# One tile for all weight buffers, plain and Strassen weights at different offsets

## The chip, the cores and the metric

The kernel runs on one core of a Trainium2 chip. The metric is the device time of one execution in microseconds; a kernel's time is the median of several runs. The engines are named as in the profile: PE multiplies matrices (its weight loads are PEld), ACT and DVE work on whole tiles, POOL is a slower third one, SP issues DMAs. Names such as L172 are lines of the kernel before, unless the text says that they are of the changed one.

## The reference

A streaming encoder of two layers, 512 tokens, width 1024, all in float32. Cut to what matters:

```python
def swiglu(x, w_gate, w_up, w_down):            # D_FF = 2816
    return (jax.nn.silu(x @ w_gate) * (x @ w_up)) @ w_down

for l in range(DEPTH):                           # DEPTH = 2
    x = x + 0.5 * swiglu(rms_norm(x, ffn1_norm[l]), ffn1_w_gate[l], ffn1_w_up[l], ffn1_w_down[l])
    h = rms_norm(x, mix_norm[l])
    p = h @ w_in[l]                              # 384 + 256 + 32 + 1024 columns
    attn = mla_group(...)                        # 8 heads, chunk-causal, low-rank q and kv
    conv = conv_group(...)                       # GLU, causal depthwise conv of 31, LayerNorm, silu
    x = x + jnp.concatenate([attn, conv], axis=-1) @ w_out[l]
    x = x + 0.5 * swiglu(rms_norm(x, ffn2_norm[l]), ffn2_w_gate[l], ffn2_w_up[l], ffn2_w_down[l])
    x = rms_norm(x, post_norm[l])
```

## The kernel before, in words

**Products in three parts.** TensorE takes the operands in a rounded form (fp32r). To keep float32's accuracy each operand is split into a high part (the rounded value) and a low part (what rounding left), and each product is three matmuls that add up in one bank: high weights by high activations (L172), high weights by low activations (L173), low weights by high activations (L174), in `mm3`. A weight tile holds 128 partitions by up to 1024 columns, that is 8 blocks of 128 by 128; each block is loaded as PE's stationary operand while the matmul before streams its activations.

**Weights.** A plain weight tile is loaded to a buffer `raw` by SP's queue, cast to the high part on ACT (L153 in `load_w`, L1117 for the first tiles), and the low part is the difference, made on DVE (L159, L1118), for the output projection on POOL or by ACT and an adding DMA. The buffers come from the pool `wpool` by tags, each tag a ring of its own: `raw` (3 buffers), `wh` (4), `wl` (4), of 4 KB a partition each. Two tiny tags, `gap0` of 16 floats and `gap1` of 32, lie between them, allocated once where the first tiles are (the expression above `half_w`). By the allocation the start bytes modulo 512 are: activations `r` 192, `raw` 192, `wh` 256, `wl` 384, and 288 for the buffers of the FFN's own pool (`xj`, `xs`, `ls`, `fr`). Any weight buffer of a kind has the same value, since all are multiples of 512 long.

**An FFN** has the gate and up columns in 11 pairs of 128 by 2. The first two pairs are plain: 512 tokens wide, `plain` and `plain_first`. The other nine go through `pair` (L418): one level of Strassen-Winograd on the 2 by 2 quarters of tokens and depth, seven products instead of eight, each 256 tokens wide. The weight sums are made on DVE in float32 (buffers `fr` and `raw`, L426 to L429) and split again: `split_into` casts on ACT (L262) and subtracts on DVE (L264); `summed` (L415) is for quarters that are used as they are, with a low part `ls` that ACT and an adding DMA make (L407, L408). Four of the seven products take `product` (three 256-wide matmuls a block, L172 to L174 by `mm3`); three take `product_joined`, where high and low activations lie side by side in a tile `xj`: one matmul of 512 columns by the high weights (L391), one of 256 by the low weights (L392), which come from `ls` or, for "t3", from `wl`. The pairs go in four chunks (2, 3, 3 and 3 pairs), each followed by its part of w_down: plain for the first chunk (weight tiles of 128 by 512) and the last (128 by 768), Strassen for the two in between (`down`, L479, whose inner `times` uses `split_into` and `summed` too). The mixing block between the FFNs is plain throughout; in its up-projections of keys and values, weights stream past stationary activations.

**What sets the order.** The program is written through a tile framework: it follows reads and writes of each buffer, and a scheduler with a simulated timeline sets each engine's order, unless the program says that one thing is issued after another (`tc.issue_after`). So the order is fixed among the Strassen products (`order["pe"]` puts each behind the one before) and in some places by names ("first", "u0" and others). Before the change neither the casts nor the low parts of weights are held in program order.

Of the kernel before, what the change touches and what calls it, by code (L numbers as in the profile page):

```python
# [7 lines left out]
FP = mybir.dt.float32  # L8
FR = mybir.dt.float32r
# [3 lines left out]
ALU = mybir.AluOpType  # L13
AX = mybir.AxisListType

P = 128
# [16 lines left out]
EPS = 1e-6  # L33
WC = 1024
GAP = 96
HS = S // 2
RING = 35
WIDE = 6
# [11 lines left out]
POOLW = "wo"  # L50
# [29 lines left out]
def encoder_kernel(ctx: ExitStack, tc: tile.TileContext, xT, consts, vecs, rgain, wgu1, wd1, wdq1,  # L80
# [6 lines left out]
    wpool = ctx.enter_context(tc.tile_pool(name="w", bufs=4))  # L87
# [4 lines left out]
    def nm(s):  # L92
        uid[0] += 1
        return f"{s}{uid[0]}"
# [21 lines left out]

    small.tile([P, GAP], FP, tag="gap", name="gap", bufs=1)
    V, A, G, T = nc.vector, nc.scalar, nc.gpsimd, nc.tensor
# [30 lines left out]
    def load_w(src, w, kind=""):  # L149
        raw = wpool.tile([P, WC], FP, tag="raw", name=nm("raw"), bufs=3)  # L150
        nc.sync.dma_start(out=raw[:, :w], in_=src)
        hi = wpool.tile([P, WC], FR, tag="wh", name=nm("wh"))
        order["cast"] = A.copy(hi[:, :w], raw[:, :w]).ins  # L153
        lo = low()
        if kind == "sum":
            A.activation(lo[:, :w], raw[:, :w], AF.Copy, scale=-1.0)
            G.dma_start(out=lo[:, :w], in_=src, accum_op=ALU.add)
            return hi, lo
        (G if kind in POOLW.split() else V).tensor_tensor(lo[:, :w], raw[:, :w], hi[:, :w].bitcast(FP),  # L159
                                                          ALU.subtract)  # L160
        return hi, lo

    def low():
        return wpool.tile([P, WC], FR, tag="wl", name=nm("wl"))

    order = {}

# [90 lines left out]

    def split_into(q, src, w=WC):

        hi = wpool.tile([P, WC], FR, tag="wh", name=nm("wh"))
        A.copy(hi[:, :w], src[:, :w])  # L262
        lo = low()
        order["lo"] = V.tensor_tensor(lo[:, :w], src[:, :w], hi[:, :w].bitcast(FP), ALU.subtract).ins  # L264
        return hi, lo

    def ffn(l, gx, norm, wgu, wd, wdq, gain, done, w0=None, halved=KD):
# [3 lines left out]
    def ffn_body(fpool, l, gx, norm, wgu, wd, wdq, gain, done, w0, halved):  # L271
# [52 lines left out]
        def operands(R):  # L324

            def joined(src):
                both = fpool.tile([P, 2, S], FR, tag="xj", name=nm("xj"), bufs=WIDE)
                A.copy(both[:, :, 0:HS], src)
                V.tensor_tensor(both[:, :, HS:S], src, both[:, :, 0:HS].bitcast(FP), ALU.subtract)
                return both  # L330
# [13 lines left out]
            for i in range(2):  # L344
                e, o = wide(quarter()), wide(quarter())
                for j in range(2):
                    for par, t in ((0, e), (1, o)):
                        m = 4 * i + 2 * j + par
                        V.scalar_tensor_tensor(t[:, j], x[:, m, :], gain[:, m:m + 1], R, ALU.mult, ALU.mult)
                        yield  # L350
                b11, b12, b21, b22 = (v[:, :, h * HS:(h + 1) * HS] for v in (e, o) for h in range(2))
                for n, src in (("b11", b11), ("b21", b21)):
# [21 lines left out]
        def product(o, w, n, start, stop):  # L374
            with tc.issue_after(order["pe"]):
                for gu in range(2):
                    for k in range(4):
                        hi, lo = X[n][k // 2]
                        t = slice(k % 2 * HS, (k % 2 + 1) * HS)
                        c = slice(gu * 512 + k * P, gu * 512 + (k + 1) * P)  # L380
                        last = mm3(o[:, gu * HS:(gu + 1) * HS], w[0][:, c], w[1][:, c], hi[:, t], lo[:, t],
                                   start and gu == 0 and k == 0, stop and k == 3, True)
            order["pe"] = last

        def product_joined(os, w, n, start):
            with tc.issue_after(order["pe"]):
                for gu, o in enumerate(os):
                    for k in range(4):
                        both = X[n][k // 2][:, k % 2]
                        c = slice(gu * 512 + k * P, gu * 512 + (k + 1) * P)  # L390
                        T.matmul(o, w[0][:, c], both, start=start and k == 0, stop=False, skip_group_check=True)  # L391
                        last = T.matmul(o[:, 0:HS], w[1][:, c], both[:, 0:HS], start=False, stop=k == 3,  # L392
                                        skip_group_check=True).ins
# [10 lines left out]
        def subtracted(w, src, n=WC):  # L404

            lo = fpool.tile([P, WC], FR, tag="ls", name=nm("ls"), bufs=2)
            A.activation(lo[:, :n], src[:, :n], AF.Copy, scale=-1.0)  # L407
            G.dma_start(out=lo[:, :n], in_=w, accum_op=ALU.add)  # L408
            return lo

        def summed(w, src, n=WC, lo=None):

            lo = subtracted(w, src, n) if lo is None else lo
            hi = wpool.tile([P, WC], FR, tag="wh", name=nm("wh"))
            A.copy(hi[:, :n], src[:, :n])  # L415
            return hi, lo

        def pair(p, quartered):  # L418
# [121 lines left out]
        for p0, p1 in CHUNKS:  # L540
# [54 lines left out]
            for m in range(halved if last else KD):  # L595
                if m in ahead:
                    pd, w = ahead[m]
# [440 lines left out]
    class Finish:  # L1038
# [37 lines left out]
        def part(self, h, src, first):  # L1076
            for t in range(2):
                i = T.matmul(self.ss[:, 2 * h + t:2 * h + t + 1], src[:, t * P:(t + 1) * P], ones[:, 0:1],
                             start=first and h == 0 and t == 0, stop=not first, skip_group_check=True)
            return i.ins  # L1080
# [26 lines left out]
    st = Stats()  # L1107
    f = gained(0, "g1", gx, first_gain)
    f(0)
    w0 = [tuple(wpool.tile([P, w], t, tag=tag, name=nm(tag), bufs=n) for t, tag, n, w in (  # L1110
        (FP, "raw", 3, WC), (FP, "gap0", 1, 16), (FR, "wh", 4, WC), (FP, "gap1", 1, 32), (FR, "wl", 4, WC)))[::2]
        for _ in range(2)]

    def half_w(q, gu):
        raw, hi, lo = (v[:, gu * 512:(gu + 1) * 512] for v in w0[q])
        nc.sync.dma_start(out=raw, in_=wgu1[0, 0, q, :, gu * 512:(gu + 1) * 512])
        A.copy(hi, raw)  # L1117
        V.tensor_tensor(lo, raw, hi.bitcast(FP), ALU.subtract)  # L1118
    for m in KS:
        if m:  # L1120
            nc.sync.dma_start(out=x[:, m, :], in_=xT[m])
# [6 lines left out]
    w0 = [w[1:] for w in w0]  # L1128
# [172 lines left out]
```

## Time and profile before

| what | value |
|---|---|
| median of 3 runs | 1783.02 us (1781.78 to 1783.49) |
| the profiled run | 1781.53 us |
| span of its trace | 1779.8 us |
| mean granted TensorE clock | 0.999 |
| PE busy | 1768.6 us, 99% |
| PEld busy | 1558.0 us, 88% |
| DVE busy | 1486.0 us, 83% |
| ACT busy | 1094.9 us, 62% |
| POOL busy | 383.3 us, 22% |

In the rows of groups, `out<-in partitions*rows x columns xcount | busy, mean ns | idle before` stands for one line and shape. A row of the timeline is start, duration, engine, line, operation, buffers and shape. Matmuls are pipelined, so durations overlap; the distance from one start to the next is what one costs. The rows of the chain of work give shares of the span by engine and by line.

### The profile page before, as it was taken

The page shows a single profiled execution, that of the slowest core. Times are in us where ns is not written, and L with a number is a line of the kernel's source. Part 1 is how long each engine was busy: PE and PEld are TensorE (multiplying, and loading weights), DVE is VectorE, ACT ScalarE, POOL GpSimd, SP SyncE. Part 2 cuts the span into 40 slices and gives each one's busy share as a digit, 9 for nine tenths or more (in the row PEclk, how much of TensorE's full clock was granted, in tenths as well). Part 3 has the DMA queues.
Part 4 walks back from the last instruction along what each step waited for, and adds up shares of the span by engine and source line. Part 5 has one row for each costly group of instructions (what it writes and reads, how often), then busy time and mean ns, then how long its engine had stood idle before and what let it go on. Part 6 is the DMA issues. An engine that isn't in the chain of part 4 may idle for free.

```text
span 1779.8 us, 29441 instructions
## 1 busy us (share of the span) xinstructions
PE 1768.6 (99%) x11430; PEld 1558.0 (88%) x11430; DVE 1486.0 (83%) x2309; ACT 1094.9 (62%) x1699; POOL 383.3 (22%) x315
## 2 busy tenths in 40 slices
PE   9999999999999999999999999999999999999998
PEld 7899999888678899999888999998976788999997
DVE  7998988588965989998779989876989559999883
ACT  5576766456953575757645757554768435757664
POOL 1000000247822000000310000002576410000002
PEclk9999999999999999999999999999999999999999
DMA  5657574324203466665426575743260125575742
GB/s 170 165 140 186 136 189 114 109 86 124 71 25 101 124 162 162 159 166 131 123 66 167 125 197 124 198 112 112 80 157 24 58 68 155 150 180 140 186 117 74
DMA packets 71947, 228.28 MB, mean 128 GB/s; under 512 B 8448, under 2 KB 9600, under 8 KB 71808
## 3 DMA queue, kind: packets, MB, share of 16 engines
q1 hardware_dynamic: 55536, 171.87, 30.5%
q0 software_dynamic: 16128, 54.53, 18.3%
q8 instruction: 89, 1.46, 0.3%
q14 instruction: 50, 0.41, 0.1%
q10 hardware_dynamic: 144, 0.00, 0.0%
HBM read 222.19 MB, written 2.10 MB: 126 GB/s over the span
## 4 chain that ended last, share of the span: by engine, by line
PE 91%; DVE 5%; ACT 2%; issue 1%; DMA 1%; SPq 0%; ACTq 0%; DVEq 0%
PE ps L172 24%; PE ps L174 24%; PE ps L173 23%; PE ps L391 11%; PE ps L392 6%; DVE cv L972 1%; PE ps L921 1%; DVE mx L880 1%; PE ps L899 1%; DVE wl L264 1%; PE ps L876 0%; PE ps L678 0%; PE ps L216 0%; PE ps L914 0%; DVE r L902 0%
## 5 line engine op out<-in xcount | busy, mean ns | idle before, releaser
L172 PE MATMUL ps<-r,wh 128*128 128x256 f32 (+1 forms) x2556 | 808.8, 320 | 1.7 <-ACT wh L1117 0.6
L173 PE MATMUL ps<-r,wh 128*128 128x256 f32 (+1 forms) x2556 | 807.4, 316 | 0.8 <-DVE r L180 0.4
L174 PE MATMUL ps<-r,wl 128*128 128x256 f32 (+1 forms) x2364 | 753.9, 321 | 0.0
L172 PEld LDWEIGHTS ps<-r,wh 128*128 128x128 f32 x2556 | 480.6, 188 | 51.0 <-issue 3.7
L173 PEld LDWEIGHTS ps<-r,wh 128*128 128x128 f32 x2556 | 480.1, 188 | 42.7 <-DVE r L180 2.5
L174 PEld LDWEIGHTS ps<-r,wl 128*128 128x128 f32 x2364 | 444.1, 188 | 38.5 <-DVE wl L159 0.7
L391 PE MATMUL ps<-xj,wh 128*128 128x512 f32 x864 | 302.5, 390 | 0.0
L153 ACT CAST wh<-raw 128x1024 fp32r<-128x1024 f32 (+3 forms) x148 | 132.4, 900 | 227.9 <-PE ps L173 140.3
L262 ACT CAST wh<-fr 128x1024 fp32r<-128x1024 f32 (+1 forms) x160 | 157.8, 986 | 103.5 <-DVE fr L428 53.2
L159 DVE TENSOR_TENSOR wl<-raw,wh 128x1024 fp32r<-128x1024 f32 (+3 forms) x132 | 142.6, 1089 | 92.5 <-ACT wh L153 91.7
L408 POOL DMA_DIRECT2D ls<-in_wgu x72 | 62.5, 868 | 724.3 <-ACT ls L407 522.5
L264 DVE TENSOR_TENSOR wl<-fr,wh 128x1024 fp32r<-128x1024 f32 (+1 forms) x160 | 182.8, 1143 | 20.2 <-ACT wh L262 20.2
L391 PEld LDWEIGHTS ps<-xj,wh 128*128 128x128 f32 x864 | 160.8, 188 | 29.1
L392 PE MATMUL ps<-xj,ls 128*128 128x256 f32 x576 | 161.3, 280 | 0.0
L978 POOL TENSOR_TENSOR y<-y,pr 128x495 f32<-128x495 f32 (+29 forms) x90 | 120.3, 1339 | 46.6 <-ACT pr L976 41.2
L262 ACT CAST wh<-raw 128x1024 fp32r<-128x1024 f32 (+1 forms) x100 | 97.9, 979 | 42.1 <-PE ps L173 21.1
L264 DVE TENSOR_TENSOR wl<-raw,wh 128x1024 fp32r<-128x1024 f32 (+1 forms) x100 | 113.8, 1138 | 11.8 <-ACT wh L262 11.2
L392 PEld LDWEIGHTS ps<-xj,ls 128*128 128x128 f32 x576 | 108.1, 188 | 0.0
L209 POOL TENSOR_TENSOR r<-r,t 128x512 f32<-128x512 f32 x45 | 75.3, 1681 | 133.3 <-ACT t L205 132.7
L407 ACT ACTIVATE ls<-fr 128x1024 fp32r<-128x1024 f32 (+1 forms) x56 | 56.1, 1001 | 73.3 <-PE ps L392 41.5
L972 DVE SCALAR_TENSOR_TENSOR cv<-m,vec,cv 128x511 f32<-128x511 f32 (+14 forms) x120 | 88.1, 734 | 4.6 <-ACT cv L968 3.0
L408 POOL DMA_DIRECT2D ls<-in_wdq x32 | 27.6, 863 | 258.6 <-ACT ls L407 258.6
(258 smaller groups left out, 2921.5 us busy)
## 6 DMA issues: line engine op xcount, KB each, us to landing
fr<-in_wgu SPq DMA_DIRECT2D x112, 512.0 KB, 4.2
ls<-in_wgu POOLq DMA_DIRECT2D x72, 512.0 KB, 6.6
raw<-in_wgu SPq DMA_DIRECT2D x62, 512.0 KB, 4.6
fr<-in_wdq SPq DMA_DIRECT2D x48, 384.0 KB, 4.7
ls<-in_wdq POOLq DMA_DIRECT2D x32, 384.0 KB, 4.9
raw<-in_wd SPq DMA_DIRECT2D x32, 384.0 KB, 3.2
raw<-in_wd SPq DMA_DIRECT2D x32, 256.0 KB, 2.8
raw<-in_wcv SPq DMA_DIRECT2D x16, 512.0 KB, 3.6
```

What stands on the lines that cost most here:

```text
L153: order["cast"] = A.copy(hi[:, :w], raw[:, :w]).ins
L159: (G if kind in POOLW.split() else V).tensor_tensor(lo[:, :w], raw[:, :w], hi[:, :w].bitcast(FP), ALU.subtract)
L172: T.matmul(o, lh, rh, start=first, stop=False, skip_group_check=free)
L173: T.matmul(o, lh, rl, start=False, stop=False, skip_group_check=free)
L174: order["mm"] = T.matmul(o, ll, rh, start=False, stop=last, skip_group_check=free).ins
L262: A.copy(hi[:, :w], src[:, :w])
L264: order["lo"] = V.tensor_tensor(lo[:, :w], src[:, :w], hi[:, :w].bitcast(FP), ALU.subtract).ins
L391: T.matmul(o, w[0][:, c], both, start=start and k == 0, stop=False, skip_group_check=True)
L392: last = T.matmul(o[:, 0:HS], w[1][:, c], both[:, 0:HS], start=False, stop=k == 3, skip_group_check=True).ins
L408: G.dma_start(out=lo[:, :n], in_=w, accum_op=ALU.add)
L972: V.scalar_tensor_tensor(acc[:, s:], u[c][:, :S - s], tap(k), acc[:, s:], ALU.mult, ALU.add)
L978: order["conv"] = G.tensor_tensor(ys[c][:, s:], ys[c][:, s:], pr[:, s:], ALU.add).ins
```

## The change

All weight buffers become parts of one tile, `weights`, of 2 × 4 × 1024 + 48 floats: four high slots, then four low slots, and 48 floats at the end. `part(j, moved)` hands out the next slot of the high (j = 0) or low (j = 1) ring. Strassen stages ask for it moved: 16 floats (64 bytes) up for high parts, 48 (192 bytes) up for low ones. Plain stages get the slot at its start. When plain follows moved in a ring, one slot is left out; a moved high part in slot 3 reaches 16 floats into low slot 0. The tiny tags `gap0` and `gap1` go.

By the allocation of the changed kernel the start bytes modulo 512 are: `r` 192, plain high and low parts 192, moved high parts 256, moved low parts 384, `raw` 384, and 288 for the FFN's own pool. So Strassen weights stand to the activations as before, plain ones no longer 64 and 192 above them but at the same value.

`in_turn(key, make)` issues each cast behind the cast before it, over plain and Strassen weights alike (key "h"), and each low part behind the one before on its engine (keys V and G).

The diff:

```diff
--- before.py
+++ after.py
@@ -33,6 +33,8 @@
 EPS = 1e-6
 WC = 1024
 GAP = 96
+WN = 4
+WOFF = 16, 48
 HS = S // 2
 RING = 35
 WIDE = 6
@@ -149,19 +151,39 @@
     def load_w(src, w, kind=""):
         raw = wpool.tile([P, WC], FP, tag="raw", name=nm("raw"), bufs=3)
         nc.sync.dma_start(out=raw[:, :w], in_=src)
-        hi = wpool.tile([P, WC], FR, tag="wh", name=nm("wh"))
-        order["cast"] = A.copy(hi[:, :w], raw[:, :w]).ins
+        hi = part(0)
+        order["cast"] = in_turn("h", lambda: A.copy(hi[:, :w], raw[:, :w]))
         lo = low()
         if kind == "sum":
             A.activation(lo[:, :w], raw[:, :w], AF.Copy, scale=-1.0)
             G.dma_start(out=lo[:, :w], in_=src, accum_op=ALU.add)
             return hi, lo
-        (G if kind in POOLW.split() else V).tensor_tensor(lo[:, :w], raw[:, :w], hi[:, :w].bitcast(FP),
-                                                          ALU.subtract)
+        e = G if kind in POOLW.split() else V
+        in_turn(e, lambda: e.tensor_tensor(lo[:, :w], raw[:, :w], hi[:, :w].bitcast(FP), ALU.subtract))
         return hi, lo
 
-    def low():
-        return wpool.tile([P, WC], FR, tag="wl", name=nm("wl"))
+    weights = wpool.tile([P, 2 * WN * WC + WOFF[1]], FR, name="weights", bufs=1)
+    used, was = [0, 0], [False, False]
+
+    def part(j, moved=False):
+
+        if was[j] and not moved:
+            used[j] += 1
+        was[j] = moved
+        i = (j * WN + used[j] % WN) * WC + (WOFF[j] if moved else 0)
+        used[j] += 1
+        return weights[:, i:i + WC]
+
+    turns = {}
+
+    def in_turn(key, make):
+
+        with tc.issue_after(turns[key]) if key in turns else nullcontext():
+            turns[key] = make().ins
+        return turns[key]
+
+    def low(moved=False):
+        return part(1, moved)
 
     order = {}
 
@@ -258,10 +280,10 @@
 
     def split_into(q, src, w=WC):
 
-        hi = wpool.tile([P, WC], FR, tag="wh", name=nm("wh"))
-        A.copy(hi[:, :w], src[:, :w])
-        lo = low()
-        order["lo"] = V.tensor_tensor(lo[:, :w], src[:, :w], hi[:, :w].bitcast(FP), ALU.subtract).ins
+        hi = part(0, True)
+        in_turn("h", lambda: A.copy(hi[:, :w], src[:, :w]))
+        lo = low(True)
+        order["lo"] = in_turn(V, lambda: V.tensor_tensor(lo[:, :w], src[:, :w], hi[:, :w].bitcast(FP), ALU.subtract))
         return hi, lo
 
     def ffn(l, gx, norm, wgu, wd, wdq, gain, done, w0=None, halved=KD):
@@ -411,8 +433,8 @@
         def summed(w, src, n=WC, lo=None):
 
             lo = subtracted(w, src, n) if lo is None else lo
-            hi = wpool.tile([P, WC], FR, tag="wh", name=nm("wh"))
-            A.copy(hi[:, :n], src[:, :n])
+            hi = part(0, True)
+            in_turn("h", lambda: A.copy(hi[:, :n], src[:, :n]))
             return hi, lo
 
         def pair(p, quartered):
@@ -1107,15 +1129,13 @@
     st = Stats()
     f = gained(0, "g1", gx, first_gain)
     f(0)
-    w0 = [tuple(wpool.tile([P, w], t, tag=tag, name=nm(tag), bufs=n) for t, tag, n, w in (
-        (FP, "raw", 3, WC), (FP, "gap0", 1, 16), (FR, "wh", 4, WC), (FP, "gap1", 1, 32), (FR, "wl", 4, WC)))[::2]
-        for _ in range(2)]
+    w0 = [(wpool.tile([P, WC], FP, tag="raw", name=nm("raw"), bufs=3), part(0), part(1)) for _ in range(2)]
 
     def half_w(q, gu):
         raw, hi, lo = (v[:, gu * 512:(gu + 1) * 512] for v in w0[q])
         nc.sync.dma_start(out=raw, in_=wgu1[0, 0, q, :, gu * 512:(gu + 1) * 512])
-        A.copy(hi, raw)
-        V.tensor_tensor(lo, raw, hi.bitcast(FP), ALU.subtract)
+        in_turn("h", lambda: A.copy(hi, raw))
+        in_turn(V, lambda: V.tensor_tensor(lo, raw, hi.bitcast(FP), ALU.subtract))
     for m in KS:
         if m:
             nc.sync.dma_start(out=x[:, m, :], in_=xT[m])
```

Each engine has the same operations before and after. Their order differs in a few places; two of them follow. In the rows, `ps_` are PE's banks, `r_`, `xs_` and `xj_` activations, `fr_` and `raw_` buffers of float32 weights, `ls_` low parts made by a DMA, and `wh_`, `wl_` or `weights` the parts of weights. The buffers' numbers differ between the kernels. Lines after the change are higher: L172 to L174 became L194 to L196, L391 and L392 became L413 and L414, L153 became L155, L262 and L264 became L284 and L286, L401 became L423, L428 became L450, L607 became L629.

The first place is the end of an FFN's last Strassen pair, where the last chunk's plain part of w_down begins (here layer 0's first FFN; the other three FFNs have the same). On PE before, the first w_down group runs ahead of the last Strassen product:

```order
L392 MATMUL ps_3368<-xj_701,ls_3518 128x256
L172 MATMUL ps_3584<-r_3118,wh_3587 128x512
L173 MATMUL ps_3584<-r_3119,wh_3587 128x512
L174 MATMUL ps_3584<-r_3118,wl_3589 128x512
L172 MATMUL ps_3584<-r_3122,wh_3587 128x512
L173 MATMUL ps_3584<-r_3123,wh_3587 128x512
```

On PE after, two matmuls of that group run, then the 24 of the last product (the first three are shown), then the rest of the group:

```order
L414 MATMUL ps_3189<-xj_668,ls_3330 128x256
L194 MATMUL ps_3393<-r_2951,weights 128x512
L195 MATMUL ps_3393<-r_2952,weights 128x512
L194 MATMUL ps_3185<-r_496,weights 128x256
L195 MATMUL ps_3185<-r_497,weights 128x256
L196 MATMUL ps_3185<-r_496,weights 128x256
```

The L196 that was third in the group has moved behind 24 matmuls of the last product. On ACT before, at the same place, casts and the copies of finished banks alternate:

```order
L435 ACTIVATE t_3424<-t_3397 128x256
L401 COPY t_3481<-ps_3367 128x512
L153 CAST wh_3587<-raw_3585 128x768
L401 COPY t_3483<-ps_3368 128x512
L153 CAST wh_3619<-raw_3617 128x768
L401 COPY e_3459<-ps_3364 128x512
L153 CAST wh_3652<-raw_3650 128x768
L454 ACTIVATE t_3543<-e_3459 128x512
L153 CAST wh_3685<-raw_3683 128x768
```

And on ACT after:

```order
L457 ACTIVATE t_3242<-t_3216 128x256
L423 COPY t_3295<-ps_3188 128x512
L423 COPY t_3297<-ps_3189 128x512
L155 CAST weights<-raw_3394 128x768
L423 COPY e_3275<-ps_3185 128x512
L155 CAST weights<-raw_3424 128x768
L476 ACTIVATE t_3354<-e_3275 128x512
L155 CAST weights<-raw_3455 128x768
L155 CAST weights<-raw_3486 128x768
```

The casts of the first three w_down tiles have each moved behind one copy or activation.

The second place is in layer 0's second FFN, where the last group of the first chunk's plain w_down is followed by the first Strassen product. PE before:

```order
L172 MATMUL ps_6498<-r_6119,wh_6501 128x512
L173 MATMUL ps_6498<-r_6120,wh_6501 128x512
L172 MATMUL ps_6527<-r_6202,wh_6532 128x256
L173 MATMUL ps_6527<-r_6203,wh_6532 128x256
L174 MATMUL ps_6498<-r_6119,wl_6503 128x512
L172 MATMUL ps_6498<-r_6130,wh_6501 128x512
```

PE after:

```order
L194 MATMUL ps_6207<-r_5850,weights 128x512
L195 MATMUL ps_6207<-r_5851,weights 128x512
L196 MATMUL ps_6207<-r_5850,weights 128x512
L194 MATMUL ps_6207<-r_5861,weights 128x512
L195 MATMUL ps_6207<-r_5862,weights 128x512
```

The first two matmuls of the Strassen product (ps_6527 before) no longer stand inside the plain group; they follow its end. On DVE before, the product's low part is made ahead of two evictions:

```order
L264 TENSOR_TENSOR wl_6534<-fr_6518,wh_6532 128x1024
L607 SCALAR_TENSOR_TENSOR x<-ps_6445,x 128x512
L607 SCALAR_TENSOR_TENSOR x<-ps_6471,x 128x512
L428 TENSOR_TENSOR fr_6518<-fr_6518,fr_6520 128x1024
L429 TENSOR_TENSOR fr_6519<-fr_6519,fr_6518 128x1024
L607 SCALAR_TENSOR_TENSOR x<-ps_6498,x 128x512
```

And on DVE after:

```order
L629 SCALAR_TENSOR_TENSOR x<-ps_6158,x 128x512
L629 SCALAR_TENSOR_TENSOR x<-ps_6182,x 128x512
L286 TENSOR_TENSOR weights<-fr_6225,weights 128x1024
L629 SCALAR_TENSOR_TENSOR x<-ps_6207,x 128x512
L450 TENSOR_TENSOR fr_6225<-fr_6225,fr_6227 128x1024
L451 TENSOR_TENSOR fr_6226<-fr_6226,fr_6225 128x1024
```

The low part has moved behind both evictions, and a third eviction, of the plain group's own bank, stands ahead of the weight sums L450 and L451.

## The prediction

> **What bounds the kernel now.** I read the engines' busy time first, then the chain that ended last, then PE's waits, then the groups by line with shapes apart, and last the timeline of PE, start by start.
>
> ```profile
> span 1779.8 us, 29441 instructions
> PE 1768.6 (99%) x11430; PEld 1558.0 (88%) x11430; DVE 1486.0 (83%) x2309; ACT 1094.9 (62%) x1699; POOL 383.3 (22%) x315
> ...
> PE 91%; DVE 5%; ACT 2%; issue 1%; DMA 1%; SPq 0%; ACTq 0%; DVEq 0%
> PE ps L172 24%; PE ps L174 24%; PE ps L173 23%; PE ps L391 11%; PE ps L392 6%; DVE cv L972 1%; PE ps L921 1%; DVE mx L880 1%; PE ps L899 1%; DVE wl L264 1%; PE ps L876 0%; PE ps L678 0%; PE ps L216 0%; PE ps L914 0%; DVE r L902 0%
> ```
>
> The matrix engine is busy for 99% of the span, and five of its lines carry 88% of the chain: the three products of mm3 (L172 to L174) and the two of product_joined (L391, L392).
>
> ```profile
> PE ps L133 <- DVE ones L129: 1.1, 1, 1.1
> PE ps L876 <- ACT r L884: 1.0, 2, 0.5
> PE ps L172 <- ACT wh L1117: 0.6, 1, 0.6
> PE ps L173 <- DVE r L180: 0.4, 1, 0.4
> ```
>
> These are all of PE's waits for other engines (total, times, longest): 3.1 us in 1779.8. There is no wait left worth removing, so a change in buffers and in the order of casts can gain only by making matmuls follow each other faster, and can lose either by making them slower or by putting a wait where none is.
>
> ```profile
> L174 PE MATMUL ps<-r,wl 128*128 128x512 f32 x852 | 334.0, 396 | 0.0
> L173 PE MATMUL ps<-r,wh 128*128 128x512 f32 x852 | 333.4, 392 | 0.0
> L172 PE MATMUL ps<-r,wh 128*128 128x512 f32 x852 | 331.3, 399 | 0.7 <-ACT wh L1117 0.6
> L391 PE MATMUL ps<-xj,wh 128*128 128x512 f32 x864 | 302.5, 390 | 0.0
> ...
> L172 PE MATMUL ps<-m,wh 128*128 128x512 f32 x16 | 6.5, 406 | 0.0
> ```
>
> Three times 852 plus three times 16 gives 2604 matmuls of 512 columns with plain weights. The mean durations (390 to 406 ns) overlap their neighbours and say little; what counts is the step from one start to the next, so I read starts. The first view is a plain stage.
>
> ```profile
> 331.26 0.39 PE L174 MATMUL ps<-r,wl 128*128 128x512 f32 x1
> 331.50 0.39 PE L172 MATMUL ps<-r,wh 128*128 128x512 f32 x1
> 331.73 0.40 PE L173 MATMUL ps<-r,wh 128*128 128x512 f32 x1
> 331.96 0.40 PE L174 MATMUL ps<-r,wl 128*128 128x512 f32 x1
> 332.20 0.39 PE L172 MATMUL ps<-r,wh 128*128 128x512 f32 x1
> ...
> 335.44 0.39 PE L174 MATMUL ps<-r,wl 128*128 128x512 f32 x1
> 335.67 0.39 PE L172 MATMUL ps<-r,wh 128*128 128x512 f32 x1
> ```
>
> From 331.50 to 335.67 there are 18 steps in 4.17 us: 231.7 ns each. Nothing waits here, and yet the steps are not alike: those that begin at an L174 (seven of them from 331.26 to 335.67) add up to 1.65 us, 235.7 ns each, and the rest are shorter. Now the other kinds of step.
>
> ```profile
> 297.12 0.28 PE L172 MATMUL ps<-r,wh 128*128 128x256 f32 x1
> ...
> 298.14 0.28 PE L172 MATMUL ps<-r,wh 128*128 128x256 f32 x1
> ...
> 299.50 0.39 PE L391 MATMUL ps<-xj,wh 128*128 128x512 f32 x1
> 299.74 0.28 PE L392 MATMUL ps<-xj,wl 128*128 128x256 f32 x1
> ...
> 302.28 0.28 PE L172 MATMUL ps<-r,wh 128*128 128x256 f32 x1
> ...
> 305.04 0.39 PE L391 MATMUL ps<-xj,wh 128*128 128x512 f32 x1
> 305.27 0.28 PE L392 MATMUL ps<-xj,ls 128*128 128x256 f32 x1
> ...
> 307.80 0.40 PE L172 MATMUL ps<-r,wh 128*128 128x512 f32 x1
> ...
> 311.05 0.28 PE L172 MATMUL ps<-xs,wh 128*128 128x256 f32 x1
> ...
> 311.52 0.28 PE L173 MATMUL ps<-xs,wh 128*128 128x256 f32 x1
> ...
> 441.86 0.39 PE L174 MATMUL ps<-wh,r 128*128 128x512 f32 x1
> ...
> 446.01 0.39 PE L174 MATMUL ps<-wh,r 128*128 128x512 f32 x1
> ```
>
> Set beside where the buffers lie in SBUF (start byte modulo 512, from the allocation: r 192, xj and xs and ls 288, wh 256, wl 384), these steps differ with the distance from the operand that streams to the weights that are loaded meanwhile. Matmuls of 256 columns from r, with weights 64 and 192 bytes above it, take 113.3 ns (9 steps, 1.02 us); from xs, with weights 32 below and 96 above, 117.5 ns (4 steps, 0.47 us). The pairs of L391 and L392 take 347.5 ns (8 pairs, 2.78 us) where L391 streams while wl is loaded from 96 bytes above xj, and 345.0 ns (8 pairs, 2.76 us) where it streams while ls is loaded from the same offset as xj. Taking off a 256-wide step of 118 leaves 229.5 and 227.0 for the 512-wide one. Where weights stream past a stationary r, 64 and 192 bytes the other way, 18 steps take 4.15 us: 230.6. The best 512-wide step in the kernel is thus 227.0, twice the best 256-wide one (226.6), and it is the only one with both operands at the same offset.
>
> **The change, part by part.** No instruction is added or removed; every engine has the same operations, the DMAs too.
>
> *Offsets.* Plain weights go from 64 (high) and 192 (low) bytes above r to the offset of r itself. Strassen weights keep 64 and 192, so the 256-wide products and the pairs of L391 and L392 should stay at 113.3, 345.0 and 347.5. What a plain 512-wide step becomes is not in the trace; the rows bound it. Best: 227.0, as L391 ahead of ls. That is 4.7 ns on 2604 matmuls, −12.2 us. Worst among rows: 235.7, as L174's steps, if meeting at one offset makes every load cost what the worst costs now: +4.0 ns, +10.4 us. I take 228.25, the middle of L391's two values, nearer to the row at the same offset than to today's plain steps, but not all of it, because L391 is followed by a 256-wide matmul each time and a plain stage never is. That is 3.45 ns × 2604 = −9.0 us. PE has no slack elsewhere (3.1 us of waits), so what the steps lose the span loses. DVE is the next engine at 1486.0 us, which leaves room. The 96 matmuls of 512 columns in which weights stream, and their narrower neighbours, change offset too: at some 3 ns either way on the 96 that is 0.3 us; with the narrower ones I allow 1 us either way in the range and nothing in the sum.
>
> In a sentence apart: the Trainium skill, page "TensorE: Matmul & The Clock Gate", Back-to-back issue gap, gives N/2.4 + 2.5 ns for matmuls in a row, 215.8 ns for 512 columns; by it the same 2604 steps could give up 41 us, but no plain step in the rows above is under 0.23 us, so I leave it out of the sum.
>
> *One slot skipped after a Strassen stage.* A plain cast that follows Strassen ones leaves out one of four slots, so it waits for a product that PE reads later. It happens at the end of all four FFNs' gate-and-up stage, where the weights for w_down are prepared.
>
> ```profile
> 302.36 0.83 ACT L153 CAST wh<-raw 128x768 fp32r<-128x768 f32 x1 [0.44 <-PE ps L391]
> ...
> 307.92 0.83 ACT L153 CAST wh<-raw 128x768 fp32r<-128x768 f32 x1 [1.48 <-issue]
> ```
>
> In the new order the first cast can start only when the t1 product is over (about 304.4, 2.0 us later) and the third only after the last product, 4.6 us later by the times of before. Behind these casts on ACT stand the copies of the next banks, which the new order puts ahead of them. Of the w_down group that PE used to run first, only two matmuls still do; the last product now fills the gap, and the group's L174 comes 24 matmuls later. The first group therefore needs its low part some 2.7 us later than before, and the second and third weights are wanted 4 us apart (18 matmuls of 0.23). I cost it at nothing, hidden by that product; without the cover it is up to 4.6 us a stage, 18 us in all.
>
> *The turn from plain to Strassen.* Moved high slot 3 overlaps the first 64 bytes of low slot 0, so there a cast waits for a plain low part to be read. One place has both live, in layer 0's second FFN.
>
> ```profile
> 611.40 1.05 ACT L262 CAST wh<-fr 128x1024 fp32r<-128x1024 f32 x1
> 613.28 1.22 DVE L264 TENSOR_TENSOR wl<-fr,wh 128x1024 fp32r<-128x1024 f32 x1
> 615.20 0.39 PE L174 MATMUL ps<-r,wl 128*128 128x512 f32 x1
> 617.28 0.51 PE L174 MATMUL ps<-r,wl 128*128 128x512 f32 x2
> ```
>
> The cast now has to wait for that L174 (about 615.0 to 615.4 in the new order, which holds the 256-wide pair back). Cast 1.05 and low part 1.22 later it is 617.7, and PE wants the low part at 617.5. Behind it on DVE stand an eviction and the sum of L428, whose cast PE wants only after two further products, 5.5 us on (24 steps of 0.113 and eight pairs). I take 0.3 us, with 0 to 1 as bounds.
>
> *Casts and low parts in program order.* Elsewhere the order moves by a few rows near the start of each FFN, with operands ready at least a microsecond ahead: nothing.
>
> Sum against the profiled run: 1781.53 − 9.0 + 0.3 = 1772.8. The median of the runs (1783.02) lies 1.5 above that run, so 1774.3, rounded to 1774.
>
> **The rivals.** *Offsets make no difference.* Then only the 0.3 us is left: 1783.3. For it: the plain steps of 229 to 236 ns show that lines with the same offsets differ, so something else works there as well. Against it: one and the same pair of instructions, L391 and L392, takes 345.0 or 347.5 by the buffer of its low weights alone. In a sentence apart: the Trainium skill's page "TensorE: Matmul & The Clock Gate", Step-by-step, says that PE reads the streaming operand and the weights through two independent ports, so that a load takes nothing from a running matmul, and by that rule this rival is the outcome; the two kinds of pair speak against it.
>
> *Slower: the same offset is the bad one in a plain stage.* A stream of equal 512-wide matmuls may settle into a rhythm in which each load meets the stream at its worst point, as L174's steps do today, every time instead of one time in three. At 235.7 that is +10.4, and with the 0.3 above 1793.7 at the median. It decides from 1.4 ns a matmul (3.6 us over 2604). For it: the best offsets for 256 columns (64 and 192) are not the best for 512, so the rhythm matters more than the distance, and no row shows a plain stage at distance 0. Against it: L391 at distance 0 is the fastest 512-wide step there is.
>
> *Slower: the late casts are exposed.* If the last product does not cover the skipped slot, PE stands up to 4.6 us at the end of each FFN, against a gain that may be small. With no gain and the full price: 1801; it outweighs the forecast's gain from half of that price on. Against it: the new order puts 24 matmuls of independent work into the gap.
>
> **How the numbers follow.** Forecast, plain steps clearly shorter: 0.55, about 1769 to 1779 of its own. No difference: 0.17. Same offset bad: 0.20. Casts exposed: 0.08. A measurement of this kernel can tell about 0.2%, 3.6 us, from no change, so faster is below 1779.5 and slower above 1786.6: 0.55, 0.17 and 0.28. The range starts at 1767: the best step on every matmul with the 1 us of the streaming weights is 1783.0 − 12.2 − 1 = 1769.8, and 3 us below it are for steps read to 10 ns and the spread of the runs (1.7); it goes up to 1790, into the third case, so that about 0.15 is left out above and 0.03 below.
>
> **What would show it.** In the timeline of a plain stage 18 steps take about 4.11 us instead of 4.17, and L174's steps are no longer the long ones; the busy time of the three plain groups falls only with the steps, so the starts are to be read, not the durations. The pairs of L391 stay at 2.76 and 2.78 us for eight, the 256-wide ones at 1.02 for nine. PE's waits stay below 5 us in all, with none over 1 us at the ends of the FFNs' Strassen stages or near 617. I am wrong if plain steps stay at 231 to 232 (first rival), lengthen (second), or if the list of PE's waits names casts (third).

## The result

| kernel | median | range | runs |
|---|---|---|---|
| before | 1782.10 us | 1781.78 to 1783.49 | 5 |
| after | 1774.52 us | 1774.20 to 1775.21 | 5 |

The ratio is 0.9956, with a 95% interval of 0.9942 to 0.9969: faster by 7.6 us, that is 0.4%, where 8.7 us were forecast. The profiled run of after took 1775.21 us.

The page of after, its span and busy time:

```profile
span 1773.2 us, 29449 instructions
...
PE 1757.9 (99%) x11430; PEld 1558.9 (88%) x11430; DVE 1488.3 (84%) x2309; ACT 1096.5 (62%) x1699; POOL 383.2 (22%) x315
```

The span is 6.6 us shorter, and PE is still the bound. A plain stage on the timeline of after (start, duration, engine, line):

```profile
328.61 0.39 PE L194 MATMUL ps<-r,weights 128*128 128x512 f32 x1
...
329.06 0.39 PE L196 MATMUL ps<-r,weights 128*128 128x512 f32 x1
329.29 0.39 PE L194 MATMUL ps<-r,weights 128*128 128x512 f32 x1
...
332.69 0.39 PE L194 MATMUL ps<-r,weights 128*128 128x512 f32 x1
```

From 328.61 to 332.69 there are 18 steps in 4.08 us, 226.7 ns each, where it was 231.7, and the step that begins at L196 (L174 before) is no longer longer than the others. On 2604 matmuls that would be −13.0 us; summed over all starts of the two traces, the steps of the 2556 plain matmuls from r cost 12.1 us less. The Strassen stages did not move:

```profile
285.82 0.28 PE L194 MATMUL ps<-r,weights 128*128 128x256 f32 x1
...
286.38 0.28 PE L196 MATMUL ps<-r,weights 128*128 128x256 f32 x1
...
305.98 0.39 PE L413 MATMUL ps<-xj,weights 128*128 128x512 f32 x1
...
308.39 0.39 PE L413 MATMUL ps<-xj,weights 128*128 128x512 f32 x1
```

Five 256-wide steps take 0.56 us (112 ns) and seven pairs with ls 2.41 us (344 ns); over the whole traces the means are 114.9 ns and 345.1 ns in both kernels. But PE's list of waits (total, times, longest) has grown from 3.1 to 7.3 us:

```profile
PE ps L196 <- DVE weights L162: 2.5, 3, 0.9
PE ps L898 <- ACT r L906: 1.5, 3, 0.5
PE ps L194 <- ACT weights L1137: 1.3, 1, 1.3
PE ps L135 <- DVE ones L131: 1.1, 1, 1.1
PE ps L879 <- DVE r L924: 0.3, 1, 0.3
PE ps L194 <- ACT weights L155: 0.3, 1, 0.3
PE ps L196 <- DVE weights L286: 0.3, 1, 0.3
```

The list has only idle stretches of more than 0.15 us. Added up from start to start, with all that is more than 60 ns above the usual step of a kind called a gap, the account closes: 12.1 us less in plain steps, 4.6 us more in gaps and 1.0 us more in other steps make the 6.6 us of the span. (A gap costs more than its row, because idle time counts from the end of the matmul before, and that overlaps the next step: below, L195 at 604.65 is followed after 1.25 us, 1.02 above a step, for a wait of 0.85.) Of the 4.2 us of new waits, 0.7 are for the first cast at the start (L1137), a wait that goes from under 0.15 to 1.7 us between the traces of the runs below, and 0.8 stand in the mixing block (L898 a third time, L879). The largest new row, L196 for the low parts of L162, has three places, near 65, 604 and 1482 us. The second of them, DVE's rows and then PE's:

```profile
603.37 0.68 DVE L351 TENSOR_TENSOR xj<-t,xj 128x512 fp32r<-128x512 f32 x1
603.97 1.28 DVE L629 SCALAR_TENSOR_TENSOR x<-ps,x 128x512 f32<-128x512 f32 x2
605.16 0.68 DVE L162 TENSOR_TENSOR weights<-raw,weights 128x512 fp32r<-128x512 f32 x1
...
604.65 0.40 PE L195 MATMUL ps<-r,weights 128*128 128x512 f32 x1
605.90 0.50 PE L196 MATMUL ps<-r,weights 128*128 128x512 f32 x1 [0.85 <-DVE weights L162]
```

The low part of a w_down tile is made last in a queue of work without a gap. Ahead of it stands the split of the last Strassen operand, L351. In the kernel before, the same stretch reads:

```profile
606.71 0.68 DVE L159 TENSOR_TENSOR wl<-raw,wh 128x512 fp32r<-128x512 f32 x1
...
607.91 0.68 DVE L329 TENSOR_TENSOR xj<-t,xj 128x512 fp32r<-128x512 f32 x1
...
607.48 0.46 PE L174 MATMUL ps<-r,wl 128*128 128x512 f32 x1
```

There the low part is done at 607.39 and used at 607.48; the split (L329) comes behind it.

### The profile page after: what moved, and what is told of

Read it like the earlier page. It is cut to its first block, busy times and chain, and to the rows that moved or that the text cites. A ratio compares the mean times of both kernels' runs of the same rounds, so it can differ in the third digit from the quotient of the medians.

```text
span 1773.2 us, 29449 instructions
## 1 busy us (share of the span) xinstructions
PE 1757.9 (99%) x11430; PEld 1558.9 (88%) x11430; DVE 1488.3 (84%) x2309; ACT 1096.5 (62%) x1699; POOL 383.2 (22%) x315
## 5 line engine op out<-in xcount | busy, mean ns | idle before, releaser
L194 PE MATMUL ps<-r,weights 128*128 128x256 f32 (+1 forms) x2556 | 805.7, 319 | 2.8 <-ACT weights L1137 1.3
L195 PE MATMUL ps<-r,weights 128*128 128x256 f32 (+1 forms) x2556 | 806.2, 316 | 0.5
L196 PE MATMUL ps<-r,weights 128*128 128x256 f32 (+1 forms) x2364 | 750.3, 319 | 2.9 <-DVE weights L162 2.5
L194 PEld LDWEIGHTS ps<-r,weights 128*128 128x128 f32 x2556 | 480.4, 188 | 48.9 <-issue 3.8
L195 PEld LDWEIGHTS ps<-r,weights 128*128 128x128 f32 x2556 | 480.4, 188 | 37.2 <-DVE r L202 2.1
L196 PEld LDWEIGHTS ps<-r,weights 128*128 128x128 f32 x2364 | 444.4, 188 | 38.5 <-DVE weights L162 3.8
L413 PE MATMUL ps<-xj,weights 128*128 128x512 f32 x864 | 302.5, 390 | 0.0
L155 ACT CAST weights<-raw 128x1024 fp32r<-128x1024 f32 (+3 forms) x148 | 131.7, 902 | 214.4 <-PE ps L195 121.3
L284 ACT CAST weights<-fr 128x1024 fp32r<-128x1024 f32 (+1 forms) x160 | 157.9, 987 | 98.5 <-DVE fr L450 50.5
L162 DVE TENSOR_TENSOR weights<-raw,weights 128x1024 fp32r<-128x1024 f32 (+3 forms) x132 | 142.6, 1088 | 80.9 <-ACT weights L155 79.6
L286 DVE TENSOR_TENSOR weights<-fr,weights 128x1024 fp32r<-128x1024 f32 (+1 forms) x160 | 182.4, 1140 | 20.8 <-ACT weights L284 20.8
L413 PEld LDWEIGHTS ps<-xj,weights 128*128 128x128 f32 x864 | 160.8, 188 | 29.1
L414 PE MATMUL ps<-xj,ls 128*128 128x256 f32 x576 | 161.3, 280 | 0.0
L284 ACT CAST weights<-raw 128x1024 fp32r<-128x1024 f32 (+1 forms) x100 | 98.0, 980 | 42.4 <-PE ps L195 21.4
L286 DVE TENSOR_TENSOR weights<-raw,weights 128x1024 fp32r<-128x1024 f32 (+1 forms) x100 | 113.5, 1135 | 11.6 <-ACT weights L284 10.9
L414 PEld LDWEIGHTS ps<-xj,ls 128*128 128x128 f32 x576 | 108.1, 188 | 0.0
```

Of the source, the lines that this page charges most:

```text
L155: order["cast"] = in_turn("h", lambda: A.copy(hi[:, :w], raw[:, :w]))
L162: in_turn(e, lambda: e.tensor_tensor(lo[:, :w], raw[:, :w], hi[:, :w].bitcast(FP), ALU.subtract))
L194: T.matmul(o, lh, rh, start=first, stop=False, skip_group_check=free)
L195: T.matmul(o, lh, rl, start=False, stop=False, skip_group_check=free)
L196: order["mm"] = T.matmul(o, ll, rh, start=False, stop=last, skip_group_check=free).ins
L284: in_turn("h", lambda: A.copy(hi[:, :w], src[:, :w]))
```

## The experiments

My theory: the distance, modulo 512 bytes, from the streamed operand to the weights that are loaded meanwhile sets the step, and the new waits come from the order. The rivals: the new order or the one tile made the steps shorter; the place of the weights counts, not the distance; high and low weights only have to agree with each other; the waits come from PE being earlier. Each kernel was run five times or more (the first eleven times), in turn with the kernel before, and ratios are to that.

**The order alone.** Plain weights back at 64 and 192; the rows of all engines stand as in after but for 2 of PE and a few of DVE, around 612 and near 950 us.

```diff
+POFF = 16, 48
-        i = (j * WN + used[j] % WN) * WC + (WOFF[j] if moved else 0)
+        i = (j * WN + used[j] % WN) * WC + (WOFF[j] if moved else POFF[j])
```

> Everything of the change but the offsets: one tile, casts and low parts in program order, the skipped slot; plain weights stand 64 and 192 bytes above the activations, as before the change (so no high slot reaches into a low one). My theory, that the distance between the streamed and the loaded operand sets the step: 18 plain steps take 4.17 us again, PE's waits stay near the 7 us of the changed kernel, about 1786 us. Rival, that one tile and the new order make the steps shorter: 4.09 us for 18 steps and 1774 to 1775 us.

1785.05 us, ratio 1.0014 (1.0005 to 1.0023). On its timeline, and in its waits:

```profile
328.83 0.39 PE L195 MATMUL ps<-r,weights 128*128 128x512 f32 x1
...
333.00 0.39 PE L195 MATMUL ps<-r,weights 128*128 128x512 f32 x1
```

```profile
PE ps L197 <- DVE weights L163: 1.6, 3, 0.9
```

18 steps take 4.17 us again. So neither the order nor the one tile shortened a step; together they cost about 2.4 us, and the three waits for low parts are there although PE is as slow as before. The three steps of a plain block are as unequal as before: over the whole trace 231.3 ns from L195, 229.3 from L196 and 234.9 from L197. The offsets by themselves are worth the way from here to after, about 10.5 us.

**The offsets without the turns.**

```diff
-        with tc.issue_after(turns[key]) if key in turns else nullcontext():
-            turns[key] = make().ins
-        return turns[key]
+        return make().ins
```

> The changed kernel without the turns: casts and low parts are left to the scheduler, offsets and skipped slot stay. If the turns cause the new waits near 65, 604 and 1482 us: 18 plain steps 4.09 us, PE's waits back to 3 to 4 us, about 1770 us (1782.1 less 12.2). If the waits come from the skipped slot or from PE being earlier: waits stay near 7 us and 1774 to 1775 us.

1787.27 us, ratio 1.0029 (1.0018 to 1.0040): neither case. Its first waits:

```profile
PE ps L194 <- DVE weights L284: 3.6, 9, 1.2
PE ps L193 <- DVE r L200: 3.3, 8, 1.0
PE ps L194 <- DVE weights L162: 2.5, 3, 0.9
```

The waits on L162 are the same as in after, so the turns don't cause them. Without the turns others come on top, 6.9 us of them in the first two rows, in the Strassen stages, and the whole is 12.8 us slower than after. The steps are those of after (plain ones 227.1 ns on average); of the 12.0 us by which the span is longer, 11.3 are gaps, nearly all in the 256-wide products. DVE's and ACT's rows stand in another order in the Strassen stages. I read it so: in one tile the scheduler is free to make casts and low parts in an order that hurts, and the turns take that freedom away; which moved row does the harm was not tried. With the one tile the turns are thus worth having; what they cost or save with the old tags no run shows.

**All weights at the offset of r.** Strassen weights at the slots' start too.

```diff
-        i = (j * WN + used[j] % WN) * WC + (WOFF[j] if moved else 0)
+        i = (j * WN + used[j] % WN) * WC
```

> The changed kernel with Strassen weights at the slots' start too, the offset of r. If a distance of 64 and 192 is right for 256 columns and wrong for 512: the 4920 matmuls of 256 columns from r go from 114 to about 118 ns, +20 us, 1793 to 1797 us; plain steps stay at 227. If the same offset is right for any width: 1774 to 1775 us or a little less.

1795.60 us, ratio 1.0073 (1.0060 to 1.0086). A 256-wide product from r:

```profile
298.15 0.28 PE L194 MATMUL ps<-r,weights 128*128 128x256 f32 x1
...
300.19 0.28 PE L196 MATMUL ps<-r,weights 128*128 128x256 f32 x1
```

17 steps take 2.04 us, 120 ns; over the whole trace the mean of such steps is 119.9 ns, where 64 and 192 gave 114.9. Of the distances run, the best depends on the width: 0 for 512 columns, 64 and 192 for 256.

This run also contradicts a part of my theory. In a joined product with ls, L413 streams xj while ls is loaded from the same offset, and neither of the two was moved; only the high weights went, from 32 bytes below xj to 96 below:

```profile
300.31 0.39 PE L413 MATMUL ps<-xj,weights 128*128 128x512 f32 x1
...
302.76 0.39 PE L413 MATMUL ps<-xj,weights 128*128 128x512 f32 x1
```

Seven pairs take 2.45 us, 350 ns, where they took 2.41 (344). Over all 576 such pairs it is 350.0 against 345.1, and most of it is the step from L413, 230.8 against 227.0, in which ls is loaded from distance 0 in both kernels. So the step is not set by the weights that are loaded during it alone; where the other weights of the stage stand counts too. The unequal steps above say the same: L195 and L197 both stream r while high weights are loaded from 64 bytes above it, and take 231.3 and 234.9.

**High and low weights alike, 64 above r.** `POFF = 16, 16` in the first diff.

> The changed kernel with plain high and low weights both 64 bytes above r (Strassen as changed). My theory, that it is the distance to r: steps of 229 to 236 ns, 18 in 4.15 to 4.2 us, 1780 to 1787 us. Rival, that high and low weights only have to have the same offset as each other: 18 steps in 4.09 us, 1774 to 1775 us.

1787.96 us, ratio 1.0031 (1.0020 to 1.0043).

```profile
328.43 0.39 PE L195 MATMUL ps<-r,weights 128*128 128x512 f32 x1
...
332.63 0.39 PE L195 MATMUL ps<-r,weights 128*128 128x512 f32 x1
```

18 steps take 4.20 us, 233.3 ns: longer than at 64 and 192, and now all three steps are alike (233.2 to 233.4). The time is 1 us above the range that I expected. That high and low agree makes the three steps equal, but not short; the rival falls.

**128 and 256 above r.** `POFF = 32, 64`, the tile 16 floats longer and the small pool's gap as much shorter.

> The changed kernel with plain high weights 128 and plain low weights 256 bytes above r. By the distance theory the steps at which high weights are loaded (those that begin at the first and third matmul) have one value, the step at which low weights are loaded another, both between 227 and 236 ns; 18 steps in 4.1 to 4.2 us, 1776 to 1788 us. If only distances below 64 or the sign count, both values are equal.

1788.07 us, ratio 1.0035 (1.0021 to 1.0048).

```profile
328.22 0.39 PE L195 MATMUL ps<-r,weights 128*128 128x512 f32 x1
...
332.42 0.39 PE L195 MATMUL ps<-r,weights 128*128 128x512 f32 x1
```

Again 4.20 us for 18, and the time is at the end of what I expected. At a resolution of 10 ns the rows don't tell the steps apart, but the means over the whole trace, of some 820 steps each, do: 232.7 ns from L195 and 234.3 from L197, which load high weights, and 232.3 from L196, which loads low ones. I had expected one value for the first two; they differ by 1.6 ns, the first and the low one by 0.4. Again the distance to the weights that are loaded meanwhile is not all.

**Everything 64 bytes higher.** The order is that of after to the row.

```diff
+    cpool.tile([P, 16], FP, name="pad")
     x = cpool.tile([P, KD, S], FP, name="x")
```

> The changed kernel with every buffer 64 bytes higher, so that all distances stay and all places change; the order is unchanged. By the distance theory nothing changes: 18 plain steps 4.09 us, 1774 to 1775 us. If the place of the weights counts (plain weights now start at 256, where the slower high weights of the kernel before stood): steps longer than 4.12 us for 18, above 1777 us.

1774.92 us, ratio 0.9958 (0.9945 to 0.9970).

```profile
328.28 0.39 PE L195 MATMUL ps<-r,weights 128*128 128x512 f32 x1
...
332.36 0.39 PE L195 MATMUL ps<-r,weights 128*128 128x512 f32 x1
```

4.08 us for 18, as in after. The weights now start where the high ones of the kernel before stood, and it makes no difference: for this shift it is how the buffers stand to each other that counts, not their place. That distances are to be taken modulo 512, and not another power of two, was not tried by itself.

**The kernel before with all weights at the offset of r.** Its order is that of before to the row, its offsets are those of the third experiment.

```diff
-GAP = 96
+GAP = 144
-        (FP, "raw", 3, WC), (FP, "gap0", 1, 16), (FR, "wh", 4, WC), (FP, "gap1", 1, 32), (FR, "wl", 4, WC)))[::2]
+        (FP, "raw", 3, WC), (FR, "wh", 4, WC), (FR, "wl", 4, WC)))
```

> The kernel before, in its own order and with its tags, but with high and low weights of all stages at the offset of r (the two gaps left out, the gap of the small pool longer, so that the FFN's own pool stays at 288). Beside the one-tile kernel with all weights at that offset (1795.6 us), which has the same offsets and the new order, it gives the price of the new order alone. If the new waits come from the order: 18 plain steps 4.09 us, PE's waits near 3 us, about 1791 to 1792 us. If they come from PE arriving earlier: waits near 7 us and 1795 to 1796 us.

1794.22 us, ratio 1.0065 (1.0052 to 1.0077), its waits:

```profile
PE ps L133 <- DVE ones L129: 1.1, 1, 1.1
PE ps L876 <- ACT r L884: 1.0, 2, 0.5
PE ps L172 <- ACT wh L1117: 1.0, 1, 1.0
PE ps L172 <- ACT wh L153: 0.6, 2, 0.3
PE ps L174 <- DVE wl L264: 0.2, 1, 0.2
```

PE is as fast in plain stages as after, and there is no wait for the low parts of w_down (L159): 3.9 us of waits in all. So those waits come with the new order, and PE being earlier only makes them longer (1.6 us with slow steps, 2.5 with fast ones). The waits in the mixing block are back to those of before as well. In time the two orders are 1.4 us apart at these offsets, less than the intervals can tell; the difference I expected was 4, and the time lies between my two cases.

**The split put back behind the low part.** The changed kernel, with the order of PE as it was; on DVE some twenty rows moved and on ACT four.

```diff
-                X["t4"].append((joined if "t4" in JOINED else halved)(t4))
+                with tc.issue_after(turns[V]):
+                    X["t4"].append((joined if "t4" in JOINED else halved)(t4))
```

> The changed kernel with one thing held: the split of the last joined operand (t4) is issued behind the low part of the latest plain weight tile, so that on DVE it no longer stands ahead of two evictions and the third w_down tile's low part; PE's order is unchanged. If that split causes PE's new waits near 65, 604 and 1482 us: the waits on L162 fall from 2.5 us to under 0.7, 1771.5 to 1773 us. If they come from PE being earlier on a busy DVE: the waits stay or move to the next low part, 1774 to 1775 us.

1773.45 us, ratio 0.9947 (0.9934 to 0.9961). DVE near 604 us, then two rows of the waits, the second the one that was 2.5:

```profile
604.09 1.88 DVE L630 SCALAR_TENSOR_TENSOR x<-ps,x 128x512 f32<-128x512 f32 x3
605.88 0.68 DVE L162 TENSOR_TENSOR weights<-raw,weights 128x512 fp32r<-128x512 f32 x1
```

```profile
PE ps L701 <- DMA r<-m: 1.3, 1, 1.3
...
PE ps L196 <- DVE weights L162: 0.3, 1, 0.3
```

The split is gone from there and most of the wait with it: the moved split is the main cause. The list shows less than is left, since it starts at 0.15 us: from L195 to L196 it is 0.71, 0.54 and 0.40 us at the three places, where it was 1.30, 1.25 and 1.09 and a step is 0.23. About 1 us of 3 is still lost there, to a DVE queue that comes late even without the split. The profiled run was this kernel's slowest (1777.24 us) and lost 1.3 us to a DMA in the mixing block (the first of the two rows), so the page says less on the time than the five runs do; by them the gain over after is about 1 us, which the intervals don't separate from nothing, and the median lies between the two cases.

**The FFN's pool at the offset of r as well.** One number; the order is that of after to the row.

```diff
-GAP = 96
+GAP = 72
```

> The changed kernel with the gap of the small pool 24 floats shorter, so that xj, xs, ls and m start at 192 as r does; the order of all engines is unchanged. By the distance theory: the 256-wide steps of L414 and of xs see weights 64 and 192 above and go from 118 to about 114 ns (1296 steps, some 5 us), L413 ahead of ls stays at distance 0 (about 227) and ahead of the moved low weights at 229; together 1768 to 1771 us. If the distance has nothing to do with these steps: 1774 to 1775 us.

1771.74 us, ratio 0.9939 (0.9927 to 0.9952). Steps from xs, then the last pair of a joined product and what follows it near 102 us:

```profile
310.75 0.28 PE L194 MATMUL ps<-xs,weights 128*128 128x256 f32 x1
...
311.32 0.28 PE L196 MATMUL ps<-xs,weights 128*128 128x256 f32 x1
...
295.51 0.39 PE L413 MATMUL ps<-xj,weights 128*128 128x512 f32 x1
...
297.89 0.39 PE L413 MATMUL ps<-xj,weights 128*128 128x512 f32 x1
...
102.12 0.28 PE L414 MATMUL ps<-xj,ls 128*128 128x256 f32 x1
...
102.44 0.19 PEld L194 LDWEIGHTS ps<-r,weights 128*128 128x128 f32 x1 [0.35 <-ACT t L423]
```

Five steps from xs take 0.57 us, 114 ns instead of 117.5, and seven pairs with ls 2.38 us, 340 ns instead of 344. So these steps follow the offsets too. Added up over the trace, the steps cost 9.2 us less; but the steps from L413 that load moved low weights got longer, 231.1 ns where it was 229.8. More than half of it is given back: where the product after a joined one writes the bank that ACT is still copying, PE now waits (0.32 us from 102.12 to the next start instead of 0.12; it is seen at 24 places, 5 us in all). The time lies just above the first case.

**Both.**

> The same with the FFN's own pool at the offset of r, as in the run with the shorter gap (1771.7 us). If both gains add: 1768 to 1770 us. If the second is given back in waits of PE for ACT's copies of a finished bank, which that run showed (24 times 0.2 us): no better than 1771 us.

1770.07 us, ratio 0.9926 (0.9913 to 0.9938), at the edge of the first case. It is the fastest of all these kernels: 4 to 5 us below the changed one by the medians, most of it from the one number of the gap.

## Why the prediction came out right, and where it did not

The median, 1774.5, is the forecast's 1774, but that it is so close is luck: two terms of the sum were wrong and went against each other, and the kernel before, put at 1783.0 by three runs, has a median of 1782.1 by five.

- *Offsets.* In the main it held: the offsets alone, without any change in order, shorten the plain steps, and 0 is the best of the four pairs of distances that were run for 512 columns. But I argued from the distance to the weights that are loaded during a step, and took L391 ahead of ls at 227.0 as what distance 0 gives; with the high weights elsewhere the same step at distance 0 takes 230.8. That all weights at the offset of r would give 227 was thus no more than a good guess. The size was off too. I took 228.25 ns, the middle of two values of L391, out of caution that a plain stage never has a 256-wide step between; the step came out at 226.7 in the rows above and 227.1 over the whole trace, as the best row I had, and the term at −12.1 us instead of −9.0.
- *The turn from plain to Strassen.* Forecast 0.3 us, with the cast released by the plain low part's matmul and the low part done just too late. The rows of after, on ACT, DVE and PE:

```profile
613.71 1.05 ACT L284 CAST weights<-fr 128x1024 fp32r<-128x1024 f32 x1 [3.51 <-PE ps L196]
...
614.79 1.22 DVE L286 TENSOR_TENSOR weights<-fr,weights 128x1024 fp32r<-128x1024 f32 x1 [1.07 <-ACT weights L284]
...
615.67 0.28 PE L195 MATMUL ps<-r,weights 128*128 128x256 f32 x1
616.07 0.39 PE L196 MATMUL ps<-r,weights 128*128 128x256 f32 x1
```

  The cast starts as the first L196 of the last plain group ends, the low part is done at 616.01, and L196 starts 0.40 us after L195, 0.28 more than a 256-wide step. Right, in cause and in size. (The row for L286 in the list of waits, 0.3 us once, is another place, a Strassen part of w_down at 1120.71; this one is too short to be listed.)
- *One slot skipped.* Costed at nothing behind the last product. The three waits on L162 lie elsewhere and at the ends of the Strassen stages no start comes later than a step. Right.
- *Casts and low parts in program order: nothing, with operands ready at least a microsecond ahead.* This step failed. The argument goes by when the moved operands are used, and not by what stood behind them on a full DVE: the low part that follows was 0.09 us early in the kernel before, the split in front of it takes 0.6 us, and three FFNs paid for it, 2.5 us in waits. Nor are the moved rows few: set side by side, the two traces have about 95 of DVE's 2309 rows and 66 of ACT's 1699 in another place, the mixing blocks included, where 0.8 us of new waits stand. In all, the gaps cost 4.6 us more, where the sum has 0.3. The sign given for being right, waits below 5 us, was missed with 7.3.
- *No difference* fell with after and the first experiment: nearly the same order at two sets of offsets has 226.7 and 231.7 ns. The Trainium skill, page "TensorE: Matmul & The Clock Gate", Step-by-step, says that a weight load takes nothing from a running matmul, because the two are read through independent ports; by that, the experiments at 0, 64 and 128 bytes would all have the same step. They have 226.7, 233.3 and 233.3, and the measurement decides. The 215.8 ns that the prediction quotes from the Trainium skill, page "TensorE: Matmul & The Clock Gate", Back-to-back issue gap, is by that section's own words the gap of an isolated matmul; the plain steps average 227.0 ns or more in every run here.
- *The same offset is the bad one* fell too: at 512 columns it is the best of the four pairs of distances that were run, at 256 columns it is worse than 64 and 192 by 5 ns.

## What to carry to other kernels

On a PE-bound kernel, read the step from one start to the next and not the busy time, and look for kinds of matmul of the same width with different steps: the buffers' offsets may be the reason, and a padding of some bytes is all it takes to try. Try whole sets of offsets and measure the stage: a step taken from one place did not keep its length when a third buffer moved. When order moves on an engine that is busy without a gap, check what stands behind the moved row, not only the row itself. A gain on the bound engine arrives short by the waits that it uncovers: here 12.1 us of steps became 6.6 us of span.

## What I had not expected of the hardware

A 512-wide fp32r step took 226.7 ns with weights at the streamed operand's offset modulo 512, 231.7 at 64 and 192 above, 233.3 at 64 and 64 and at 128 and 256; a 256-wide one 119.9 at 0 and 114.9 at 64 and 192, by the means of whole traces. So the favourable distance changes with the width. And a step depends on more than the operand that streams and the weights that are loaded meanwhile: with both at the same offset it took 227.0 or 230.8 by where the other weights of the stage stand. What in the reading of the operands makes it so, none of these runs shows.
